# Row normalisation on one core: the last four tiles stored in pairs with 64 KB packets, some rows scaled singly

## The chip, the cores and the metric

The kernel runs on one core of one Trainium2 chip. The metric is the device time of one execution in microseconds (us), lower is better. Runs are compared by their medians.

## The reference

```python
# x: float32, 32 x 512 x 1024
sums = np.sum(np.abs(x), axis=-1, keepdims=True)
return (x / (sums + 1e-8)).astype(np.float32)
```

Each row of 1024 numbers is divided by the sum of its absolute values. There are 16384 rows, 67.1 MB in and as many out.

## The kernel before

The rows are cut into 16 tiles of 1024 rows. A tile puts 8 rows on each of 128 partitions, 32 KB per partition and 4 MB in all. On-chip memory holds six tiles at a time in one buffer `x_all`; tile i lies in slot i mod 6 (`cell`, line 45). The scaled rows overwrite the loaded ones.

Three queues carry the work. SP issues every load (line 52), ScalarE's queue (ACT) issues every store (line 57), and both feed the same 16 DMA engines. VectorE (DVE) does nearly all the arithmetic. The order on each is the order in which the program is written, since the schedule is manual (line 94): a waiting instruction holds up all that is behind it on its engine.

At the start five loads are issued: tiles 0, 1, 2, 3 singly and 4 and 5 in one transfer (lines 95 to 97). Then the loop runs over groups (line 33): tile 0, tile 1, the pairs (2, 3) to (12, 13), tile 14, tile 15. For each group VectorE sums the absolute values of all its rows (`tensor_reduce`, line 65), adds 1e-8 (line 72), takes the reciprocal (line 74) and multiplies the rows by it in one instruction (`tensor_mul`, line 80). In tiles 0 and 15 VectorE multiplies four of the eight rows and ScalarE the other four, one `activation` each (line 87). Then every tile of the group is stored, and the load of the tile six further on is issued, which waits until the store has emptied its slot.

A transfer is cut into packets of at most `max_dma_last_dim` bytes: 32 KB (`WHOLE`), that is one partition's share of a tile. Tile 0 is stored in two transfers: rows 0 and 1 of each partition in 4 KB packets, rows 2 to 7 in 24 KB packets.

Of the kernel before, what the change touches and what calls it, by code (L numbers as in the profile page):

```python
# [1 line left out]

# [4 lines left out]

FP32 = mybir.dt.float32
EPS = 1e-8


@with_exitstack
def kernel(
    ctx: ExitStack,
    tc: tile.TileContext,
    x: bass.AP,
    out: bass.AP,
):
    nc = tc.nc
    P = nc.NUM_PARTITIONS  # L20

    x_flat = x.flatten_outer_dims()
    out_flat = out.flatten_outer_dims()
    n, d = x_flat.shape

    R, SLOTS = 8, 6
    WHOLE = 4 * R * d
    LEAD = 2
    count = n // (P * R)
    assert n == P * R * count and count % 2 == 0  # L30
    last = count - 1

    groups = [(0, 1), (1, 1)] + [(i, 2) for i in range(2, last - 1, 2)] + [(last - 1, 1), (last, 1)]

    joint = SLOTS - 2

    sbuf = ctx.enter_context(tc.tile_pool(name="sbuf", bufs=1))
    stats = ctx.enter_context(tc.tile_pool(name="stats", bufs=len(groups)))
    x_all = sbuf.tile([P, SLOTS * R, d], FP32, name="x_all")

    def piece(flat, i, tiles=1):
        a = P * R * i
        return flat[a : a + P * R * tiles, :].rearrange("(t p r) d -> p t r d", t=tiles, p=P)

    def cell(i, a=0, b=R):
        lo = R * (i % SLOTS)
        return x_all[:, lo + a : lo + b, :]

    def load(i, tiles=1):
        lo = R * (i % SLOTS)  # L50
        dst = x_all[:, lo : lo + R * tiles, :].rearrange("p (t r) d -> p t r d", t=tiles)
        nc.sync.dma_start(out=dst, in_=piece(x_flat, i, tiles), max_dma_last_dim=WHOLE)  # L52

    def store(i):
        parts = [(0, LEAD, 4 * d), (LEAD, R, WHOLE)] if i == 0 else [(0, R, WHOLE)]
        for a, b, size in parts:
            nc.scalar.dma_start(
                out=piece(out_flat, i)[:, 0, a:b, :],
                in_=cell(i, a, b),
                max_dma_last_dim=size,  # L60
            )

    def factors(i, w):
        s = stats.tile([P, 2 * R], FP32)
        nc.vector.tensor_reduce(  # L65
            out=s[:, :w],
            in_=cell(i, 0, w),
            axis=mybir.AxisListType.X,
            op=mybir.AluOpType.add,
            apply_absolute_value=True,  # L70
        )
        nc.vector.tensor_scalar_add(out=s[:, :w], in0=s[:, :w], scalar1=EPS)  # L72
        inv = stats.tile([P, 2 * R], FP32)
        nc.vector.reciprocal(out=inv[:, :w], in_=s[:, :w])  # L74
        return inv

    def scale(i, w, inv):

        kv = R // 2 if i in (0, last) else w
        nc.vector.tensor_mul(  # L80
            out=cell(i, 0, kv),
            in0=cell(i, 0, kv),
            in1=inv[:, :kv].unsqueeze(2).to_broadcast([P, kv, d]),
        )
        for r in range(kv, w):
            row = cell(i, r, r + 1)[:, 0, :]
            nc.scalar.activation(  # L87
                out=row,
                in_=row,
                func=mybir.ActivationFunctionType.Copy,  # L90
                scale=inv[:, r : r + 1],
            )

    with tc.manual_schedule():
        for i in range(joint):
            load(i)
        load(joint, 2)
        for first, tiles in groups:
            scale(first, R * tiles, factors(first, R * tiles))
            for i in range(first, first + tiles):  # L100
                store(i)
                if i + SLOTS < count:
                    load(i + SLOTS)


# [1 line left out]
_INS = ['x']  # L107
_OUTS = [((32, 512, 1024), 'float32')]


# [23 lines left out]
```

## Time and profile before

| what | value |
|---|---|
| median of 3 runs (lowest to highest) | 316.48 us (316.48 to 316.99) |
| the profiled execution, whole | 316.37 us |
| its span, from the first to the last instruction | 314.4 us |
| VectorE busy | 271.2 us in 40 instructions |
| ScalarE busy | 9.8 us in 9 |
| DMA | 134.22 MB in 4864 packets |
| transfers | 15 loads, 17 stores |

Engines are called DVE (VectorE), ACT (ScalarE), POOL (GpSimd) and SP; a q behind the name is that engine's queue of DMA issues. L80 is line 80 of the kernel. In the queues' packets and transfers, "landed" is when the last of the 16 engines has reported its share done. A transfer of 4 MB is 8 packets of 32 KB on each of the 16 DMA engines. Of the 4864 packets 512 are 4-byte completion packets, 16 to a transfer. Multiplied or summed, a group's duration depends on its shape, so the text names the shape with it: 17.2 us for 128x16384 elements, 8.7 for 128x8192, 4.4 for 128x4096.

### The profile page before, as it was taken

To read this page: it belongs to the slowest core of one execution; us is meant where nothing else is said; L and a number is where in the kernel's file an instruction comes from. 1 tells how busy PE (TensorE), PEld (TensorE's weight loads), DVE (VectorE), ACT (ScalarE), POOL (GpSimd) and SP (SyncE) were. 2 spreads that over 40 slices of the span, in tenths; PEclk is the share of its full clock that TensorE was granted. 3 is DMA by queue.
4 is the path that set the end of the run, shared out by engine and by line. 5 is a ranking of instruction groups with operands and counts; after the bars stand their busy time and mean duration, and the time that the engine had idled before them with its cause. 6 is when DMAs were issued, how large, how long until landed. Compare 5 with 4: busy or idle time off the path is not lost.

```text
span 314.4 us, 165 instructions
## 1 busy us (share of the span) xinstructions
DVE 271.2 (86%) x40; ACT 9.8 (3%) x9; POOL 0.2 (0%) x4
## 2 busy tenths in 40 slices
DVE  0399999999999999999799977999689999999500
ACT  0113000000000000000000000000000000000500
POOL 0000000000000000000000000000000000000000
DMA  8999999999999999999999999999999999999997
GB/s 333 404 463 404 459 401 427 418 425 467 400 467 400 467 400 467 400 467 400 467 400 467 400 467 400 467 400 467 400 463 404 459 408 459 409 459 409 459 409 333
DMA packets 4864, 134.22 MB, mean 427 GB/s; under 512 B 512, under 2 KB 512, under 8 KB 768
## 3 DMA queue, kind: packets, MB, share of 16 engines
q1 hardware_dynamic: 2288, 67.11, 49.8%
q10 hardware_dynamic: 2576, 67.11, 49.5%
HBM read 67.11 MB, written 67.11 MB: 427 GB/s over the span
## 4 chain that ended last, share of the span: by engine, by line
DVE 47%; DMA 40%; another core or an unknown queue 6%; issue 0%; SPq 0%; DVEq 0%
DVE x_all L80 25%; DVE s L65 22%; DMA out_dram<-x_all 21%; DMA x_all<-in_x_dram 19%; DVE inv L74 0%; DVE s L72 0%; SPq L52 0%; DVEq L65 0%
## 5 line engine op out<-in xcount | busy, mean ns | idle before, releaser
L65 DVE TENSOR_REDUCE s<-x_all 128x16 f32<-128x16384 f32 (+1 forms) x10 | 138.0, 13801 | 23.1 <-DMA x_all<-in_x_dram 23.1
L80 DVE TENSOR_TENSOR x_all<-x_all,inv 128x16384 f32<-128x16384 f32 (+2 forms) x10 | 129.6, 12958 | 0.3
L87 ACT ACTIVATE x_all<-x_all,inv 128x1024 f32<-128x1024 f32 x8 | 8.5, 1138 | 272.2 <-DVE inv L74 272.2
L74 DVE RECIPROCAL inv<-s 128x16 f32<-128x16 f32 (+1 forms) x10 | 2.3, 233 | 0.3
L72 DVE TENSOR_SCALAR s<-s 128x16 f32<-128x16 f32 (+1 forms) x10 | 1.7, 173 | 0.3
L87 ACT ACT_TABLE_LOAD x1 | 1.3, 1283 | 13.1 <-DMA x_all<-in_x_dram 13.1
L118 POOL MEMSET const-bfloat16-1.0<- 128x1 bf16 x1 | 0.1, 101 | 0.0
L118 POOL MEMSET const-uint8-127<- 128x1 uint8 x1 | 0.1, 101 | 0.0
L118 POOL MEMSET const-float32-0.0<- 128x1 f32 x1 | 0.1, 98 | 0.2 <-issue 0.2
L118 POOL MEMSET const-float32-1.0<- 128x1 f32 x1 | 0.1, 98 | 0.0
## 6 DMA issues: line engine op xcount, KB each, us to landing
out_dram<-x_all ACTq DMA_DIRECT2D x15, 4096.0 KB, 37.5
x_all<-in_x_dram SPq DMA_DIRECT2D x14, 4096.0 KB, 24.2
x_all<-in_x_dram SPq DMA_DIRECT2D x1, 8192.0 KB, 71.4
out_dram<-x_all ACTq DMA_DIRECT2D x1, 3072.0 KB, 43.2
out_dram<-x_all ACTq DMA_DIRECT2D x1, 1024.0 KB, 25.4
```

The costliest lines, as they stand in the source:

```text
L65: nc.vector.tensor_reduce(out=s[:, :w], in_=cell(i, 0, w), axis=mybir.AxisListType.X, op=mybir.AluOpType.add, apply_absolute_value=True,)
L72: nc.vector.tensor_scalar_add(out=s[:, :w], in0=s[:, :w], scalar1=EPS)
L74: nc.vector.reciprocal(out=inv[:, :w], in_=s[:, :w])
L80: nc.vector.tensor_mul(out=cell(i, 0, kv), in0=cell(i, 0, kv), in1=inv[:, :kv].unsqueeze(2).to_broadcast([P, kv, d]),)
L87: nc.scalar.activation(out=row, in_=row, func=mybir.ActivationFunctionType.Copy, scale=inv[:, r : r + 1],)
L118: nc = _bacc.Bacc("TRN2", target_bir_lowering=False, num_devices=1)
```

## The change

- The six first tiles are loaded by six transfers.
- Tiles 12 to 15 are laid out in pairs: of a block of 2048 rows each partition holds 16 consecutive ones, the first 8 in the first tile of the pair. Each tile is still loaded by itself. Both are stored together in one transfer with packets of up to 64 KB, after the second of them.
- Tile 0's rows 0 and 1 are stored by a transfer each.
- Groups of tiles 2 to 11 are multiplied 8 rows at a time, so in two instructions. Group (12, 13) is multiplied as before.
- In tile 14 VectorE multiplies four rows and ScalarE four, as in tiles 0 and 15 before.
- In tiles 0 and 15 VectorE multiplies its four rows one by one with `tensor_scalar_mul`.

```diff
-    joint = SLOTS - 2
+    paired = count - 4
...
     def piece(flat, i, tiles=1):
         a = P * R * i
-        return flat[a : a + P * R * tiles, :].rearrange("(t p r) d -> p t r d", t=tiles, p=P)
+        return flat[a : a + P * R * tiles, :].rearrange("(p r) d -> p r d", p=P)
...
-    def load(i, tiles=1):
-        lo = R * (i % SLOTS)
-        dst = x_all[:, lo : lo + R * tiles, :].rearrange("p (t r) d -> p t r d", t=tiles)
-        nc.sync.dma_start(out=dst, in_=piece(x_flat, i, tiles), max_dma_last_dim=WHOLE)
+    def load(i):
+        if i < paired:
+            src = piece(x_flat, i)
+        else:
+            h = i % 2
+            src = piece(x_flat, i - h, 2)[:, R * h : R * (h + 1), :]
+        nc.sync.dma_start(out=cell(i), in_=src, max_dma_last_dim=WHOLE)
 
     def store(i):
-        parts = [(0, LEAD, 4 * d), (LEAD, R, WHOLE)] if i == 0 else [(0, R, WHOLE)]
-        for a, b, size in parts:
+        if i == 0:
+            parts = [(i, 0, 1, 4 * d), (i, 1, LEAD, 4 * d), (i, LEAD, R, WHOLE)]
+        elif i < paired:
+            parts = [(i, 0, R, WHOLE)]
+        else:
+            parts = [(i - 1, 0, 2 * R, 2 * WHOLE)] if i % 2 else []
+        for j, a, b, size in parts:
+            tiles = 2 if j >= paired else 1
             nc.scalar.dma_start(
-                out=piece(out_flat, i)[:, 0, a:b, :],
-                in_=cell(i, a, b),
+                out=piece(out_flat, j, tiles)[:, a:b, :],
+                in_=cell(j, a, b),
                 max_dma_last_dim=size,
             )
...
-        kv = R // 2 if i in (0, last) else w
-        nc.vector.tensor_mul(
-            out=cell(i, 0, kv),
-            in0=cell(i, 0, kv),
-            in1=inv[:, :kv].unsqueeze(2).to_broadcast([P, kv, d]),
-        )
+        kv = R // 2 if i in (0, last - 1, last) else w
+        if i not in (0, last):
+            step = kv if i >= paired else R
+            for a in range(0, kv, step):
+                nc.vector.tensor_mul(
+                    out=cell(i, a, a + step),
+                    in0=cell(i, a, a + step),
+                    in1=inv[:, a : a + step].unsqueeze(2).to_broadcast([P, step, d]),
+                )
+        else:
+            for r in range(kv):
+                row = cell(i, r, r + 1)[:, 0, :]
+                nc.vector.tensor_scalar_mul(out=row, in0=row, scalar1=inv[:, r : r + 1])
...
-        for i in range(joint):
+        for i in range(SLOTS):
             load(i)
-        load(joint, 2)
```

## The prediction, as put on record

> **What bounds the kernel now.** I read the page's DMA part first, because every byte goes in once and out once: 134.22 MB.
>
> ```profile
> span 314.4 us, 165 instructions
> ...
> DVE 271.2 (86%) x40; ACT 9.8 (3%) x9; POOL 0.2 (0%) x4
> ...
> DMA  8999999999999999999999999999999999999997
> GB/s 333 404 463 404 459 401 427 418 425 467 400 467 400 467 400 467 400 467 400 467 400 467 400 467 400 467 400 467 400 463 404 459 408 459 409 459 409 459 409 333
> DMA packets 4864, 134.22 MB, mean 427 GB/s; under 512 B 512, under 2 KB 512, under 8 KB 768
> ```
>
> All 16 DMA engines are busy in every slice but the first and last. VectorE (DVE) is also 86% busy, so I asked for the busy time by stretch, to see where the DMA engines rest.
>
> ```profile
> core 0: us, DVE busy (x) ACT busy (x) POOL busy (x), PEclk, DMA share, GB/s
> 0.00:1.70 1.70, 0.00 (x0) 0.00 (x0) 0.20 (x4) 1.00 0.00 0
> ...
> 2.70:313.30 310.60, 271.15 (x40) 9.82 (x9) 0.00 (x0) 1.00 1.00 430
> 313.30:314.40 1.10, 0.00 (x0) 0.00 (x0) 0.00 (x0) 1.00 0.00 0
> ```
>
> The DMA share is 0.00 for 1.7 us, 1.00 for 310.6 us, and 0.00 for the last 1.1 us. This is the bound: the 16 engines never rest between their first and last packet. The page's chain of waits seems to say otherwise:
>
> ```profile
> DVE 47%; DMA 40%; another core or an unknown queue 6%; issue 0%; SPq 0%; DVEq 0%
> ```
>
> It gives VectorE 47%, because it steps from a wait to its releaser and cannot see that a transfer waits in a queue behind other packets. I go by the windows.
>
> How long is one packet? In the trace's packet records a 32 KB packet takes 1.213 us, the next starting 1.209 us after it; a 24 KB packet takes 0.912 and a 4 KB one 0.159. These lie on one line, 37.65 ns per KB plus 8.4 ns each. Direction makes no difference: at the end, with stores alone, tiles 11 to 15 land at 274.93, 284.62, 294.28, 303.96 and 313.63, one per 9.68 us; in the middle, with loads and stores mixed, stores 6 to 9 land at 185.35, 204.68, 224.08 and 243.40, a load and a store per 19.35 us, again 9.68 each. So only fewer bytes, cheaper packets or less rest at the ends could make this kernel faster, and only a gap in the queues could make it slower. The place where a gap could open is the end, which the timeline shows:
>
> ```profile
> 229.03 17.22 DVE L65 TENSOR_REDUCE s<-x_all 128x16 f32<-128x16384 f32 x1 [3.74 <-DMA x_all<-in_x_dram]
> ...
> 263.92 8.68 DVE L65 TENSOR_REDUCE s<-x_all 128x8 f32<-128x8192 f32 x1
> 264.03 18.10 ACTq L57 DMA_DIRECT2D out_dram<-x_all  x3
> ...
> 273.07 8.69 DVE L80 TENSOR_TENSOR x_all<-x_all,inv 128x8192 f32<-128x8192 f32 x1
> 281.68 8.68 DVE L65 TENSOR_REDUCE s<-x_all 128x8 f32<-128x8192 f32 x1
> ...
> 290.84 4.43 DVE L80 TENSOR_TENSOR x_all<-x_all,inv 128x4096 f32<-128x4096 f32 x1
> 290.84 4.27 ACT L87 ACTIVATE x_all<-x_all,inv 128x1024 f32<-128x1024 f32 x4 [264.40 <-DVE inv L74]
> 295.35 0.34 ACTq L57 DMA_DIRECT2D out_dram<-x_all  x1
> ```
>
> Columns are start, duration, engine, line. The reader is to see that tile 15 is handed to its store at 295.35, while store 14 keeps the engines busy until it lands at 303.96: 8.6 us of cover. VectorE at the end costs nothing now.
>
> **The change, part by part.**
>
> *Six loads instead of five, tile 0's store in three instead of two.* Bytes and packets of data stay. Each adds an issue (0.33 to 0.62 us on SP and on ACT) and 16 completion packets of 4 bytes; the two joined stores below save as many, so 32 transfers stay 32. On SP the issue falls under load 0, in flight until 12.99. On ACT the first store stays behind tile 0's four activations, at about 26.6, and the third goes out near 27.5 instead of 27.1; loads 3 to 5 fill the engines until 74. A completion packet takes a turn of its store queue: in the packet records tile 0's 24 KB packets start about 1.4 us after the completion packets ahead of them. Store 0, and load 6 behind it on SP, may so be up to 1.4 us later, while the engines work for the other queue. I take 0; up to 1.4 us could reach VectorE's last chain, below.
>
> *Groups 2 to 10 scaled in two multiplications of 8 rows.* Five groups, each 2 x 8.69 in place of 17.22: 0.16 us more, 0.8 in all. VectorE waits 2.56, 3.76 and 3.74 us for loads ahead of groups 8, 10 and 12, which swallows it; without that cover it would delay the last chain by 0.8. The first store of each pair can issue 8.6 us earlier. That is worth nothing: when store 6 issues at 149.05, store 5 is still queued ahead of it and lands only at 165.95. So stores land, and the loads behind them on SP start, as before.
>
> *Eight rows (four of tile 0, four of tile 15) scaled singly.* The trace has no such instruction. The same kind (TENSOR_SCALAR) on 16 elements takes 0.17 us, a floor. The multiplication grows by 1.04 ns per element, (8692 - 4426)/4096, plus 0.16 us, so 1.23 us for 1024 elements is a ceiling. Four rows: 0.7 to 4.9 us, against 4.43 now. ScalarE's four rows beside them take 4.27 either way. Of the ends I take those 4.27 us as what decides, and keep +0.6 for the ceiling. The Trainium skill (VectorE: DVE Perf Modes, The perf-mode tier table) gives this kind in float32 two elements per cycle where the multiplication has one, 1.23 us for 2048 elements; by it, an estimate, four rows take under 4.27 and the ceiling is out. No row here shows it, and the sum stands without it.
>
> *Loads of tiles 12 to 15 from a double tile, stores of two tiles in 64 KB packets.* A load keeps 32 KB packets, each from an address 64 KB after the last partition's, not 32 KB. I cost this at nothing: store 0's second part already writes 24 KB out of every 32 KB, with packets on the line above. The stores have 128 packets of 64 KB in place of 256 of 32 KB, 16 fewer per engine over both pairs. Each packet saved is worth between 1.209 less the line's 1.205 for the bytes, 4 ns, and the full 8.4 ns: 0.07 to 0.13 us. I take 0.07, since 1.209 is the pace at which packets really follow each other. Nothing is late next; it is engine time.
>
> *Store 14 waits for tile 15; ScalarE scales half of tile 14.* Store 12 and 13 leave together at 264.03 as before (group 12 is still one multiplication) and their last packets end, like store 13's now, between 293.6 and 293.9 (first and last completions 293.96 and 294.28, less the 0.33 us between the last packet's end at 313.30 and its landing at 313.63). By then the joined store must be in the queue; store 14 issued at 281.80 and now issues with store 15. VectorE: the half of tile 14 takes 4.43 (form 128x4096) and the next reduction can start 4.34 after it starts, as after tile 0 (22.18 to 26.52): 277.41 in place of 281.68, 4.27 earlier. All that follows moves by 4.27: the last scaling from 290.84 to 286.57, the issue from 295.35 to 291.1. From issue to first packet with an idle queue the trace shows 1.0 us (0.73 to 1.73). So packets are ready at 292.1, 1.5 us before the first engine runs dry. ScalarE's new 4.27 us at 273.07 delays no one: its next duty is tile 15. The cost is nothing while the 1.5 us hold.
>
> **Sum.** The profiled execution took 316.37 us, 314.4 of span and 1.97 around it. Minus 0.07 gives **316.3**. The median of the runs shown is 316.48 (316.48 to 316.99), so this is 0.06% below it. A measurement of this kernel can tell about 0.2%, 0.6 us, from no change; I forecast no difference.
>
> **Rivals.**
>
> *A gap before the last store (slower).* Place: the joined store's issue on ACT. It decides from an issue later than 292.6 (293.6 less 1.0). For it: 4.27 us of VectorE time has to be saved to pay for 9.3 us of lateness, and the spare is 1.5 us; the 1.4 of the completion packet and the 0.6 of the ceiling add up to 2.0, a gap of 0.5. A queue that starts from empty pays more: the first packets of the run took up to 2.21 us instead of 1.21, which adds 1.0. So 1.5 us, 317.8. If nothing were saved on VectorE, 295.35 + 1.0 - 293.6 is 2.7, or 319.0. Against it: load 13, at which the last chain starts, comes out of two queues that are both full, whatever store 0 did. Chance of over 0.6 us: 0.13.
>
> *The wider spacing in memory slows the transfers (slower).* Four tiles in and out are 8 x 9.68 = 77 us of engine time, so each per cent costs 0.8 us; two per cent give 317.9. Against it are store 0's packets on the line. The Trainium skill (DMA: Bandwidth & Descriptors, Latency and other measured facts) has copies slow down at spacings that are large powers of two, from 214 to 207 GB/s at 512 KB; that 3%, an estimate, would give 318.8, but its spacing is eight times that of here, and no run here shows it. Chance 0.05.
>
> *Cheaper packets (faster).* To pass 0.6 us, each of the 16 joins has to save 40 ns, five times the 8.4 of the line: 315.7. For it: nothing but that no 64 KB packet has been seen. Chance 0.06.
>
> *The packets are cut to 32 KB after all.* Then 316.37, not to be told from the forecast. Chance 0.06, and 0.70 for the forecast itself.
>
> Hence faster 0.06, same 0.76, slower 0.18. The range reaches from a gain of 0.4 to a gap of 1.2 us, 315.9 to 317.5, with 0.06 left out below and 0.12 above.
>
> **What would show it.** Packets of 4608 instead of 4864 (256 fewer) if the 64 KB hold. The joined store issued at 291.1 or before. A DMA share of 1.00 in the windows from 264 to 313; a gap would be a fall between 293 and 296. Groups of loads and stores still landing 9.68 us apart. First stores of pairs issued 8.6 us earlier and landing no earlier. I am wrong if the issue comes after 292.6, or if the 64 KB packets take other than 2.41 us.

## The result

The changed kernel takes 317.97 us (median of 6 runs, 317.75 to 318.07), the kernel before 316.72 (6 runs): a ratio of 1.0036, 95% interval 1.0025 to 1.0047. It is slower, by 0.36%, and lies 0.5 us above the forecast range.

The same rows of the page that the prediction shows of the kernel before, here of the changed kernel: the span, the busy time of the engines, the DMA row and the packets.

```profile
span 316.4 us, 177 instructions
...
DVE 264.1 (83%) x51; ACT 14.1 (4%) x13; POOL 0.2 (0%) x4
...
DMA  8999999999999999999999999999999999999996
...
DMA packets 4608, 134.22 MB, mean 424 GB/s; under 512 B 512, under 2 KB 512, under 8 KB 768
```

VectorE has 7 us less to do and the packets fell to 4608, the number that 64 KB packets should give. The span still grew by 2 us in the profiled execution. The 40 slices of 8 us hide where this happens; the DMA view of 290 to 300 us shows it. Each digit there is a quarter of a microsecond, and the digits stand where packets start:

```profile
DMA  0000099096000000000000900000000090000000
```

The 64 KB packets follow one another at 2.41 us, about ten digits. The group from 291.25 to 292.5 should be followed by one from 293.7 to 294.9. The next starts come at 295.5. In the packet records the 16 engines end their packets between 293.77 and 294.70, and the next packets begin between 295.57 and 295.72: a pause of at least 0.87 us for each engine, 1.56 on average. In the rest of the execution the pauses sum to less than 0.1 us on the mean engine. So the loss is one gap ahead of the joint store of tiles 14 and 15. This is the timeline that leads to it:

```profile
232.89 17.22 DVE L75 TENSOR_REDUCE s<-x_all 128x16 f32<-128x16384 f32 x1 [3.69 <-DMA x_all<-in_x_dram]
...
267.90 0.34 ACTq L67 DMA_DIRECT2D out_dram<-x_all  x1
...
276.94 4.27 ACT L104 ACTIVATE x_all<-x_all,inv 128x1024 f32<-128x1024 f32 x4 [250.36 <-DVE inv L84]
281.28 8.68 DVE L75 TENSOR_REDUCE s<-x_all 128x8 f32<-128x8192 f32 x1
...
290.44 4.26 ACT L104 ACTIVATE x_all<-x_all,inv 128x1024 f32<-128x1024 f32 x4 [9.23 <-DVE inv L84]
290.44 2.74 DVE L101 TENSOR_SCALAR x_all<-x_all,inv 128x1024 f32<-128x1024 f32 x4
294.73 0.34 ACTq L67 DMA_DIRECT2D out_dram<-x_all  x1
```

From the last pair's reduction to the last issue it is 61.8 us, against 66.3 before: the chain did shrink, by 4.5 us where 4.27 was forecast. But the chain starts at 232.89 instead of 229.03, because load 13 lands 3.85 us later. The issue comes at 294.73, not at 291.1. Why load 13 is late is the question.

A first answer lies at tile 0. Timeline of the kernel before, then of the changed one, from 20 to 30 us:

```profile
22.18 4.27 ACT L87 ACTIVATE x_all<-x_all,inv 128x1024 f32<-128x1024 f32 x4 [7.83 <-DVE inv L74]
...
26.63 0.95 ACTq L57 DMA_DIRECT2D out_dram<-x_all  x2
```

```profile
22.31 1.15 ACT L104 ACTIVATE x_all<-x_all,inv 128x1024 f32<-128x1024 f32 x1 [7.83 <-DVE inv L84]
22.31 2.74 DVE L101 TENSOR_SCALAR x_all<-x_all,inv 128x1024 f32<-128x1024 f32 x4
...
23.10 0.37 ACTq L67 DMA_DIRECT2D out_dram<-x_all  x1
23.36 1.13 ACT L104 ACTIVATE x_all<-x_all,inv 128x1024 f32<-128x1024 f32 x1
23.76 0.34 ACTq L67 DMA_DIRECT2D out_dram<-x_all  x1
24.41 2.17 ACT L104 ACTIVATE x_all<-x_all,inv 128x1024 f32<-128x1024 f32 x2
```

The view of the kernel before is the first one. In the program all four activations stand ahead of the stores. Yet the store of row 0 is issued at 23.10, while the first activation runs, as soon as VectorE has row 0 ready. Before, the first store had waited for VectorE's multiplication, which ended at 26.60, and not for ScalarE, which was done at 26.44. The Trainium skill (Advanced Engine Details and Errata, Sequencer and Instruction Queues) says that an engine's instructions are pushed into a queue and that the sequencer goes on reading; the trace agrees, with an issue 0.26 us before the second activation starts.

**Theory A**: stores that start 3.5 us sooner share the DMA engines with the first loads sooner. **Rival B**: loads 4 and 5, now separate, are issued at 13.14 and 22.84 (before, together at 2.67), and come later for that, or because they are two transfers. **Rival C**: the 64 KB packets or the wider spacing cost time.

### The profile page after: what moved, and what is told of

Its sections match the earlier page's. It is cut to its first block, busy times and chain, and to the rows that moved or that the text cites. A ratio compares the mean times of both kernels' runs of the same rounds, so it can differ in the third digit from the quotient of the medians.

```text
span 316.4 us, 177 instructions
## 1 busy us (share of the span) xinstructions
DVE 264.1 (83%) x51; ACT 14.1 (4%) x13; POOL 0.2 (0%) x4
## 2 busy tenths in 40 slices
DMA packets 4608, 134.22 MB, mean 424 GB/s; under 512 B 512, under 2 KB 512, under 8 KB 768
## 4 chain that ended last, share of the span: by engine, by line
DMA 49%; DVE 36%; another core or an unknown queue 6%; ACT 1%; issue 0%; SPq 0%; DVEq 0%
DMA out_dram<-x_all 27%; DMA x_all<-in_x_dram 23%; DVE s L75 22%; DVE x_all L93 12%; ACT x_all L104 1%; DVE x_all L101 1%; DVE inv L84 0%; DVE s L82 0%; SPq L56 0%; DVEq L75 0%
## 5 line engine op out<-in xcount | busy, mean ns | idle before, releaser
L93 DVE TENSOR_TENSOR x_all<-x_all,inv 128x8192 f32<-128x8192 f32 (+2 forms) x13 | 116.8, 9017 | 0.3
L104 ACT ACTIVATE x_all<-x_all,inv 128x1024 f32<-128x1024 f32 x12 | 12.8, 1137 | 267.4 <-DVE inv L84 267.4
L101 DVE TENSOR_SCALAR x_all<-x_all,inv 128x1024 f32<-128x1024 f32 x8 | 5.5, 750 | 0.1
```

The lines of the kernel that those rows point to most:

```text
L93: nc.vector.tensor_mul(out=cell(i, a, a + step), in0=cell(i, a, a + step), in1=inv[:, a : a + step].unsqueeze(2).to_broadcast([P, step, d]),)
L101: nc.vector.tensor_scalar_mul(out=row, in0=row, scalar1=inv[:, r : r + 1])
L104: nc.scalar.activation(out=row, in_=row, func=mybir.ActivationFunctionType.Copy, scale=inv[:, r : r + 1],)
```

## Experiments

Each kernel below was timed in five rounds beside the kernel before. "Span" is the median from the first to the last instruction, "outside" the rest of the time; "group 12" is when the last pair's reduction starts. The span of the kernel before has a median of 314.7 to 314.8 in the three sets of runs.

| kernel | first store | group 12 | last issue | engines dry | span | outside | ratio (95%) |
|---|---|---|---|---|---|---|---|
| before | 26.63 | 229.03 | 295.35 | 0 | 314.8 | 1.93 | 1 |
| changed | 23.10 | 232.89 | 294.73 | 1.56 | 316.3 | 1.65 | 1.0036 (1.0025 to 1.0047) |
| tile 0 in one | 26.58 | 229.30 | 291.13 | 0 | 314.7 | 2.20 | 1.0003 (0.9994 to 1.0011) |
| joined load | 23.19 | 231.62 | 293.46 | 0.53 | 314.9 | 1.97 | 1.0001 (0.9993 to 1.0010) |
| last two apart | 22.93 | 232.68 | 294.52 | 0 | 315.2 | 1.60 | 0.9994 (0.9984 to 1.0004) |
| tile 0 alone | 23.10 | 231.53 | 297.85 | 0 | 314.7 | 2.19 | 1.0006 (0.9995 to 1.0018) |
| rows reversed | 24.99 | 230.35 | 292.19 | 0 | 314.5 | 1.64 | 0.9982 (0.9974 to 0.9991) |
| two stores | 23.59 | 232.56 | 294.41 | 1.59 | 316.3 | 1.64 | 1.0039 (1.0026 to 1.0051) |
| pairs alone | 26.96 | 230.11 | 296.44 | 3.59 | 317.2 | 2.14 | 1.0089 (1.0066 to 1.0111) |
| pairs in 32 KB | 22.85 | 232.88 | 294.72 | 1.70 | 316.5 | 1.60 | 1.0042 (1.0025 to 1.0058) |

Times of issue and the dry time are those of the profiled execution. The dry time is the pause before the last store, as the mean of the 16 engines; the packet records do not name the engine, so a packet is put down to the one whose last packet ends as this one starts. "Load lag", further down, is how much later than in the kernel before a load's last packets end: the mean of the last 16, with all load packets put in the order in which they end and 128 of them counted as a load.

**Tile 0 in one multiplication** (the changed kernel):

```diff
-        if i not in (0, last):
-            step = kv if i >= paired else R
+        if i != last:
+            step = min(kv, R) if i < paired else kv
```

> The changed kernel with one part undone: VectorE multiplies its four rows of tile 0 in one instruction again. Theory A (early stores): in the changed kernel row 0 of tile 0 is stored from 23.10 us, 3.5 us sooner than before, its packets share the DMA engines with the loads sooner, and load 5 and all loads after it land 3.85 us later, so the last store is late. Then here the first store issues at about 26.6, load 13 lands at 229 to 230.3, the last store issues at 291 to 292.4, no gap, and the time is that of the kernel before within 0.3 us (316.3 to 317.0). Rival B (late issues): loads 4 and 5, issued at 13.14 and 22.84 in place of one joined load at 2.67, push the loads back; then load 13 still lands at 232.8 and the time stays at 317.9. Rival C (64 KB packets or the wider spacing cost time): the gap may go, but the time stays over 317.

Timeline of this kernel:

```profile
22.12 4.42 DVE L93 TENSOR_TENSOR x_all<-x_all,inv 128x4096 f32<-128x4096 f32 x1
...
26.58 1.36 ACTq L67 DMA_DIRECT2D out_dram<-x_all  x3
```

The first store is back at 26.58, group 12 at 229.30, the last issue at 291.13, and no engine pauses. With 316.87 us the loss is gone, with six loads, 64 KB packets and the wider spacing all still there. That is what A said; B and C alone cannot give it.

**Joined load** (the changed kernel with tiles 4 and 5 in one load):

```diff
-        for i in range(SLOTS):
+        for i in range(SLOTS - 2):
             load(i)
+        nc.sync.dma_start(
+            out=x_all[:, R * 4 : R * 6, :].rearrange("p (t r) d -> p t r d", t=2),
+            in_=x_flat[P * R * 4 : P * R * 6, :].rearrange("(t p r) d -> p t r d", t=2, p=P),
+            max_dma_last_dim=WHOLE,
+        )
```

> The changed kernel with the other early part undone: tiles 4 and 5 are loaded by one transfer again. Theory A: the loads still fall behind, load 13 lands at 232 to 233, the last store issues at 294 to 295, time 317.7 to 318.1. Rival B: the joined load goes out at 2.7 and load 13 lands at 229, no gap, 316.4. Rival C: as the changed kernel, 317.9.

A's numbers fail here. The joined load itself is issued at 13.23, so the late issue of rival B is not tested by it, yet group 12 starts at 231.62, 1.27 us sooner than in the changed kernel:

```profile
231.62 17.22 DVE L75 TENSOR_REDUCE s<-x_all 128x16 f32<-128x16384 f32 x1 [3.68 <-DMA x_all<-in_x_dram]
```

That is one packet (1.209). One transfer fewer has one set of completion packets fewer, and each of these uses a turn of its queue, in which the other queue sends a packet. The packet records show it. In the changed kernel a 4-byte packet of the load queue stands alone between two 24 KB store packets on all 16 engines, at 58.0 to 59.1 us, where load 4 ends; with the joined load there is none. The load lag at load 4 is 2.3 us in both kernels, and at load 5 it is 4.2 in the changed kernel and 3.0 here. So a second cause exists, as large as a packet: the part of rival B that says "because they are two". With it gone the gap is 0.53 and the time 316.90. In tile 0 in one, the sixth load and the third store add a turn to each queue, and group 12 moved by only 0.27: the two nearly cancel.

**Last two apart** (the changed kernel, tiles 14 and 15 stored by themselves):

```diff
+        if i >= last - 1:
+            h = R * (i % 2)
+            nc.scalar.dma_start(
+                out=piece(out_flat, last - 1, 2)[:, h : h + R, :],
+                in_=cell(i),
+                max_dma_last_dim=WHOLE,
+            )
+            return
```

> The changed kernel, but tiles 14 and 15 are stored by a transfer each with 32 KB packets; tiles 12 and 13 are still stored together in 64 KB packets, and the layout of all four stays. Theory A: the loads are still 3.85 us late, but store 14 issues at about 281 and bridges the engines until tile 15 is ready at 294.7; no gap, 316.2 to 316.8. Rival B says the same of the time. Rival C: 64 KB packets remain in one pair and the spacing in both, so at least half of the loss stays, 317.2 or more.

The loads are as late as in the changed kernel (group 12 at 232.68) and the last issue is at 294.52, but store 14 goes out at 281.24 and no engine pauses: 316.77. Late loads open no gap without the joint last store. The time is that of the kernel before with the help of 0.3 us less outside the span; the median span is still 0.4 us longer (315.2 against 314.8). In the profiled execution the last packets end only 0.16 us later on the mean engine (313.28 against 313.12) but 0.40 later on the last one (313.70 against 313.30), so one engine trails the rest; why stays open. Rival C's 317.2 did not come.

**Tile 0 alone** (the kernel before with tile 0's rows scaled singly and its store in three):

```diff
-        parts = [(0, LEAD, 4 * d), (LEAD, R, WHOLE)] if i == 0 else [(0, R, WHOLE)]
+        parts = [(0, 1, 4 * d), (1, LEAD, 4 * d), (LEAD, R, WHOLE)] if i == 0 else [(0, R, WHOLE)]
...
+        if i == 0:
+            for r in range(kv):
+                row = cell(i, r, r + 1)[:, 0, :]
+                nc.vector.tensor_scalar_mul(out=row, in0=row, scalar1=inv[:, r : r + 1])
...
```

> The kernel before, with only tile 0 changed: its four VectorE rows scaled singly and its store cut into three transfers. Theory A: the first store issues at 23.1, load 13 lands 3.5 to 4 us later than 228.94, store 15 issues near 299 instead of 295.35, and nothing is lost, since store 14 lands only at 304: 316.4 to 316.9. Rival B: load 13 lands at 229 to 230, since the joined load is kept; same time. Rival C: same time.

Group 12 moves 2.5 us, to 231.53, with the joined load kept, and not the 3.5 to 4 expected; the time does not move. The shift is A's in kind, and smaller by the turn that the third store gives the loads. The load lag from load 6 on is 2.40 us here and 2.38 in the kernel with the joined load, which has the same five loads and three stores.

**Rows reversed** (the changed kernel, tile 0's rows scaled in the order 3, 2, 1, 0):

```diff
-            for r in range(kv):
+            for r in (reversed(range(kv)) if i == 0 else range(kv)):
```

> The changed kernel with VectorE scaling its four rows of tile 0 in the order 3, 2, 1, 0, so that the first store (row 0) can go out only after all four, at about 25.1 us instead of 23.1; nothing else moves. Theory A (the loads fall behind by as much as the stores start early, with a turn of the queue more or less for each transfer): 1.5 us early in place of 3.5, so load 13 lands at 230.4 to 231 instead of 232.8, the last store issues at 292.2 to 292.9, a gap of 0 to 0.3, and the time is 316.6 to 317.1. Rival (it is the single rows themselves, not when the store goes out): load 13 at 232.8, gap 1.5, 317.9.

Its timeline, at tile 0 and at the end:

```profile
24.99 0.37 ACTq L67 DMA_DIRECT2D out_dram<-x_all  x1
25.35 1.13 ACT L104 ACTIVATE x_all<-x_all,inv 128x1024 f32<-128x1024 f32 x1
```

```profile
287.90 4.27 ACT L104 ACTIVATE x_all<-x_all,inv 128x1024 f32<-128x1024 f32 x4 [9.23 <-DVE inv L84]
287.90 2.74 DVE L101 TENSOR_SCALAR x_all<-x_all,inv 128x1024 f32<-128x1024 f32 x4
292.19 0.34 ACTq L67 DMA_DIRECT2D out_dram<-x_all  x1
```

This tests A by its size: first stores at 26.58, 24.99 and 23.10 put group 12 at 229.30, 230.35 and 232.89, with the same loads and stores. It is not one for one: by the packet records the first store packets start 2.1 and 4.0 us sooner than with tile 0 in one, and the loads end 1.1 and 3.4 us later, up to a packet less. The last issue at 292.19 is 0.4 before the 292.6 from which a gap was forecast, and there is none. In the DMA view from 290 to 300 us the groups of starts follow each other at 2.25 to 2.5 us:

```profile
DMA  0000099000000099000000009900000000990000
```

**Two stores** (the changed kernel with rows 0 and 1 in one transfer):

```diff
-            parts = [(i, 0, 1, 4 * d), (i, 1, LEAD, 4 * d), (i, LEAD, R, WHOLE)]
+            parts = [(i, 0, LEAD, 4 * d), (i, LEAD, R, WHOLE)]
```

> The changed kernel, but tile 0's rows 0 and 1 are stored by one transfer again; it goes out when row 1 is ready, at about 23.8 instead of 23.1. Theory A with turns (each transfer's completion packet takes a turn of its queue, which a packet of the other queue uses): the store queue loses a turn, so the loads fall a packet further behind, about 1.2 us, less the 0.7 us by which the store is later: load 13 lands at 233.0 to 233.6, the gap grows to 1.8 to 2.3, time 318.1 to 318.6. Rival (only the time of issue counts): load 13 lands 0.7 earlier, at 232.1, gap 0.9, 317.3.

Neither number came: group 12 at 232.56, gap 1.59, 317.98. By the packet records tile 0's first packets start 0.9 us later on the mean engine (28.2 against 27.3), where the issue is 0.5 later, so the later start and the lost turn (1.2) nearly cancel: a sum of +0.3, against -0.3 by group 12 and -0.05 by the load lag. The difference, a third to half of a packet, stays unexplained. Load 4 was issued at 2.65 here instead of 13.14, and nothing came sooner: the late issue of rival B is harmless.

**Pairs alone** (the kernel before with the paired layout and joint stores; the part in `store` is shown, and the loads read the same layout):

```diff
+    paired = count - 4
...
+        if i >= paired:
+            if i % 2:
+                a = P * R * (i - 1)
+                nc.scalar.dma_start(
+                    out=out_flat[a : a + 2 * P * R, :].rearrange("(p r) d -> p r d", p=P),
+                    in_=cell(i - 1, 0, 2 * R),
+                    max_dma_last_dim=2 * WHOLE,
+                )
+            return
```

> The kernel before with the paired layout, 64 KB packets and joint stores of tiles 12 to 15 alone; the arithmetic and tile 0 as before. Theory A: load 13 lands at 229 as before, the last store issues at 295.4, its packets start 0.95 us later, and the engines are dry from 293.8: a gap of 2.4 to 2.6, time 318.8 to 319.3. Rival C (something else in the pairs costs time as well): over 319.5.

The median is 319.34. The profiled execution took 320.29: there group 12 started 1.1 us later than before, the issue came at 296.44 and the gap was 3.59; in the three runs at 319.34 the span is about 1 us shorter. That the gap is so much smaller there, as A has it, is argued, since there is no trace of them; why the loads came a packet late in the profiled execution stays open. Without VectorE's savings the joint store costs 2.5 us of median span. Timeline of the profiled execution:

```profile
291.92 4.43 DVE L96 TENSOR_TENSOR x_all<-x_all,inv 128x4096 f32<-128x4096 f32 x1
...
296.44 0.34 ACTq L65 DMA_DIRECT2D out_dram<-x_all  x1
```

**Pairs in 32 KB** (the changed kernel with `WHOLE` in place of `2 * WHOLE`):

> The changed kernel with 32 KB packets in the joint stores; layout, transfers and waits as in the changed kernel. If the 64 KB packets save or cost nothing: the same gap of 1.5 and 317.7 to 318.1. If they save the 0.07 to 0.13 us that was forecast, the time is that much over the changed kernel, which this cannot tell; if they cost time, the time is below 317.6.

The same issue (294.72), a gap of 1.70, 318.11. The packet size is not the loss. In the packet records of the changed kernel 64 KB packets start 2.414 us apart ahead of the gap, 4 ns less than twice 1.209, and 2.42 behind it.

Reversed rows came out below the kernel before, which I had not aimed at, so three more runs asked whether that holds and where it comes from: the same kernel again, reversed rows with the last two stores apart, and the kernel before with only tile 0 changed and its rows reversed.

> The kernel with reversed rows once more, since it came out 0.18% below the kernel before: about 0.3 us of that lay outside the span of the program's instructions and 0.2 in the span. If that holds: 316.0 to 316.3, a ratio of 0.998 to 0.999. If it was chance: a ratio whose interval takes in 1.

> Reversed rows, and tiles 14 and 15 stored by a transfer each. Theory A: with reversed rows the engines do not run dry before the joint store, so parting it gains nothing: within 0.3 us of the run with reversed rows, in the span 314.4 to 314.9. If a part of the gap is still in the run with reversed rows, this is faster.

> The kernel before, with only tile 0 changed as in the changed kernel, its four rows scaled singly in the order 3, 2, 1, 0. Theory A: loads later by about 0.5 to 1.5 us (five loads, three stores, first store at about 25), which costs nothing, since store 14 keeps the engines busy: a span of 314.5 to 315.0. If the single rows of tile 0 were what lowered the time outside the span to 1.6 us, it is 1.6 here too and the time 316.2; if it is the six loads together with them, it is 2.0 or more and the time 316.7.

| kernel | time | span | outside | ratio (95%) |
|---|---|---|---|---|
| rows reversed, again | 316.19 | 314.6 | 1.60 | 0.9987 (0.9976 to 0.9998) |
| reversed, last two apart | 316.21 | 314.6 | 1.62 | 0.9987 (0.9979 to 0.9996) |
| before, tile 0 reversed | 316.90 | 314.7 | 2.19 | 1.0009 (1.0000 to 1.0018) |

It holds: 0.13 to 0.18% below the kernel before, and parting the last two stores adds nothing, so no gap is left in it. Of the 0.5 us, 0.2 lie in the span and 0.3 outside. In the third kernel group 12 starts at 229.22, 0.2 later than before, where I had expected 0.5 to 1.5: the 1.7 us of earlier issue (24.96 against 26.63) and the third store's turn cancel almost wholly. Its time outside is 2.19, so single rows alone do not lower that.

## Why the prediction was wrong, point by point

- *The bound* was right: no engine pauses in any of the profiled executions but in the gap (the rest sums to under 0.1 us on the mean engine), and every kernel without a gap is within 0.2% of the kernel before.
- *"On ACT the first store stays behind tile 0's four activations, at about 26.6"*: this step failed. It went out at 23.10. The timeline of before had shown that the first store left 0.03 us after VectorE's multiplication; I put it down to ScalarE, which had ended 0.16 us sooner, at 26.44.
- *"Load 13 ... comes out of two queues that are both full, whatever store 0 did"* failed with it. Both queues are full, but their order had been set by then. Counted on the mean engine, store packets begin at 27.3 in place of 31.1, so each engine has sent about three load packets fewer (3.8 / 1.209) when the sharing begins. The third store's turn, which gives the loads a packet, and the sixth load's, which costs them one, nearly cancel. What the loads have lost by then stays lost: the load lag is 0.4 us at load 3, 2.3 at load 4, 4.2 at load 5, and 3.60 at every load from 6 to 15, to within 0.01. In the other kernels it is just as constant from load 6 on: 0.18 with tile 0 in one, 1.30 with reversed rows, 2.38 with the joined load. The chain of waits shows load 13 in the kernel before, the changed kernel and reversed rows; columns are start and duration:

```profile
204.69 24.24 DMA x_all<-in_x_dram
```

```profile
203.12 29.67 DMA x_all<-in_x_dram
```

```profile
203.63 26.63 DMA x_all<-in_x_dram
```

Load 13 is issued 1.6 us sooner, since the stores are ahead, and is under way 5.4 us longer. The Trainium skill (DMA: Bandwidth & Descriptors, Queues, rings and completion order) states that a DMA engine takes turns between queues that have work, packet by packet; the trace of before agrees: the 16 packets of 4 KB per engine in tile 0's first store start at 31.12 on the mean engine and land at 52.01, 20.9 us, where 16 turns with a load packet between them make 16 x (1.209 + 0.159) = 21.9, the same to within a packet.
- *The six loads, the three stores*: costed at 0. The 1.4 us that were kept for a completion packet were for the third store's, as a delay; it works the other way, since its turn goes to the loads. The completion packet of the sixth load, for which no cost was kept, is the one that holds the loads up: 1.27 us between the changed kernel and the joined load.
- *Two multiplications per pair*: 17.29 to 17.30 us in place of 17.22, 0.07 more, not 0.16; hidden, as forecast.
- *Single rows*: four take 2.74 us, inside the 0.7 to 4.9. ScalarE's 4.26 decides, as taken. The Trainium skill's two elements per cycle (VectorE: DVE Perf Modes, The perf-mode tier table) agree with it: by them, an estimate, 0.61 us a row, and 2.74 / 4 = 0.69 here.
- *64 KB packets*: 4 ns per join ahead of the gap, the low end, 0.07 us in all if it held throughout; no run can tell it in the time. Wider spacing: no cost was found, since tile 0 in one has it and loses nothing (ratio 0.9994 to 1.0011).
- *The end*: the chain, 61.8 us against the forecast 62.1; issue to first packet 0.8 to 1.0 us; engines dry from 293.77 on. All right.
- *The rival "a gap before the last store"* had the right place. It was given 0.13, because the start of the last chain was thought fixed. That its price came true (a gap of 1.5 us and 317.8 written down, 1.56 and 317.97 measured) is luck. It was made of 0.5 for lateness beyond the spare and 1.0 for slow first packets. But the single rows were not slow (2.74 us, where 4.9 was the ceiling), and the first packets behind the gap took 2.46 us where the others took 2.42. The lateness was the 3.85 us of load 13, which the rival did not have.
- *The sum*: the span's median rose by 1.5 us, as the gap says. The time outside it fell from 1.93 to 1.65, which the forecast held constant, so the time rose by 1.25 only.

## What to carry to other kernels

In a kernel like this one, whose DMA engines never rest, moving a store forward takes turns from the loads, and what the loads lost early was still missing at the last one: ask of each earlier issue, and of each transfer more, whose packets it displaces. A joint last store is free only while the work it waits for ends before the engines run dry; here the margin forecast was 1.5 us, and a 3.5 us earlier first store at the other end of the kernel used it up. To say when a store goes out, look for what it waits for, and not only at the arithmetic ahead of it on the same engine's list.

## What the runs showed of the hardware that was not expected

- ScalarE's queue issued a store at 23.10 while the first of four activations that stand ahead of it was running until 23.46. The issues kept their order among themselves: with reversed rows, row 1 was scaled by 24.30, but its store went out at 25.40, behind row 0's at 24.99.
- The time outside the span is steady for a kernel to 0.1 us and differs between kernels: 1.60 to 1.65 in the changed kernel and five like it, 1.93 and 1.97 in the kernel before and the joined load, 2.14 to 2.20 in four others. What sets it was not tried and stays open; it is over half of what reversed rows gain.
- A gap of 0.53 us (joined load) cost 0.1 us of median span. On the mean engine of the profiled executions it is paid in full: the last packets end at 313.75 us, against 313.12 in the kernel before. But the 16 engines, having paused together, end together (last packets within 0.17 us there, within 0.34 in the kernel before and 1.55 in tile 0 alone). That stragglers lengthen the median span of kernels without a gap, and so hide the rest, is argued, not shown.
